# Hybrid decoder layer on one core: the last two pairs' expert rows summed on TensorE, the row planes loaded ahead of the last pair

## Chip, cores and metric

One core of a Trainium2 chip runs the whole layer in one launch. The metric is the device time of one execution in microseconds, as the median of several runs; less is better.

## What is computed

The layer takes x (512 tokens x 1024), mixes it by dilated attention and a spatial gating unit, projects and normalises it (LN1), and then runs a mixture of 32 experts of which each token uses two. The part around the change is the last line of the loop body:

```python
moe = hierarchical_moe(h, w_group, b_group, w_expert, b_expert, w_gate_up, w_down)
h = layer_norm(DEEPNORM_ALPHA * h + moe, ln2_g, ln2_b)
...
act = jax.nn.silu(a) * b * gate[:, g, :, None]
y = y + jnp.einsum('tef,efd->td', act, w_down[g])
```

So every token's output is LN2 of its own h plus the rows of its two experts, each weighted by its gate.

## The kernel before

Everything is float32. Experts are taken two at a time: 16 **pairs** (p = 0 to 15, `LAST` = 15), each with up to 64 tokens per expert, so that a pair fills 128 partitions. The tokens are four **tiles** of 128 (`NT`), and x, already normalised by LN1 and centred, stays in `x_sb`.

For each pair the loop (L1160 to L1209) does this. Its tokens' rows are gathered from `h_dram` into SBUF (POOL's indirect DMA, `gather`). TensorE transposes them (`transposed`) and multiplies them by the gate and up weights (`gate_up`, L905). ScalarE and VectorE form the gated activation `sa` (`gated`); TensorE transposes it and ScalarE copies it to `aT` (`act_transposed`); TensorE multiplies it by the down weights (`down`, L1112). The result y (128 slots x 1024) is copied out of PSUM by ScalarE with its row sums, centred on VectorE (L1121), and scattered by POOL's indirect DMA (L1122) into `y_dram`, which holds two planes of 512 rows: each token's first and second expert.

The last pair is not scattered. Its rows go to their tokens by a product: `one_hot(p)` (L1073) builds on POOL a 0/1 matrix G with one column per token, and `fin_y` multiplies G by y on TensorE in float32r (one instruction a product in the trace, where float32 has two). To keep the digits, y is split into a high half (ScalarE's copy) and a low half (VectorE's difference, L1117), and both are multiplied.

The weights come as 96 transfers of 1 MB, six a pair (four of gate/up, two of down), on SyncE's queue in order, into a ring of 21 buffers (`home(c)`, `wfill`). A transfer waits for the release of its buffer, and each DMA on this queue also waits for the landing of the one eight before it. Late in the kernel, buffers that have no next weight are used for other things: for ln2's gain and bias (`ln2`), for the planes (`rb`), for G and the low half (`spare`), for the outputs (`o_sb`).

ln2's gain and bias are spread over the partitions by small products (L1206) with ScalarE copies (L1208) in pairs 13 and 14, ahead of `act_transposed`.

**The end** (from L1211): the two planes are loaded back, eight transfers of 512 KB (L1216), after pair 14's scatter has landed. For each tile i and column half n, PSUM bank `fin[i, n]` collects: x by a product with the identity (`fin_x`, float32, L1158), pair 15's rows (`fin_y`, L1238), and the planes' rows, added up on POOL (L1244) and brought in by another identity product (`fin_rows`, L1245). The rows' means come from small products of G with the row sums `rs` (L1274). Then LN2: ScalarE squares with an accumulator (L1252), VectorE scales twice (L1257, L1264), SyncE stores (L1265). The order on each engine in this part is the order in which the code is written. A branch behind it serves experts with more than 64 tokens.

## Time and profile before

| What | Value |
|---|---|
| median of 3 runs | 501.38 us (501.13 to 502.98) |
| the profiled execution's own time | 501.38 us |
| its span, first to last instruction | 499.70 us |
| mean granted TensorE clock | 0.981 of full speed |
| TensorE products busy | 468.3 us (94%) |
| VectorE / ScalarE / POOL busy | 231.0 / 162.4 / 129.2 us |
| DMA | 141.18 MB, mean 283 GB/s |

The span is what the engines' instructions cover; the time of an execution holds 1.68 us more. Busy shares are means over stages that differ. In the last 60 us, which the change touches, only the rows by stage, the chain of waits and the landings of DMAs tell what sets the end.

### The profile page before, as it was taken

The page shows a single profiled execution, that of the slowest core. Times are in us where ns is not written, and L with a number is a line of the kernel's source. Part 1 is how long each engine was busy: PE and PEld are TensorE (multiplying, and loading weights), DVE is VectorE, ACT ScalarE, POOL GpSimd, SP SyncE. Part 2 cuts the span into 40 slices and gives each one's busy share as a digit, 9 for nine tenths or more (in the row PEclk, how much of TensorE's full clock was granted, in tenths as well). Part 3 has the DMA queues.
Part 4 walks back from the last instruction along what each step waited for, and adds up shares of the span by engine and source line. Part 5 has one row for each costly group of instructions (what it writes and reads, how often), then busy time and mean ns, then how long its engine had stood idle before and what let it go on. Part 6 is the DMA issues. An engine that isn't in the chain of part 4 may idle for free.

```text
span 499.7 us, 6653 instructions
## 1 busy us (share of the span) xinstructions
PE 468.3 (94%) x2322; PEld 280.8 (56%) x2322; DVE 231.0 (46%) x598; ACT 162.4 (33%) x366; POOL 129.2 (26%) x196
## 2 busy tenths in 40 slices
PE   7999999999899999987999999999998898799994
PEld 5788887888767678867843333333333233243351
DVE  3586637723477638798452222222234331010146
ACT  4543536241478632322112222222221121032243
POOL 4024345000296910344111211111110110000380
PEclk9999999999999999998899999999999999898998
DMA  8844231750298549585589999999999999998464
GB/s 262 288 125 114 63 121 42 221 200 0 65 402 254 190 161 364 201 282 245 169 324 378 428 419 419 419 420 422 421 420 419 420 426 419 419 423 373 151 241 171
DMA packets 40805, 141.18 MB, mean 283 GB/s; under 512 B 10508, under 2 KB 14656, under 8 KB 28993
## 3 DMA queue, kind: packets, MB, share of 16 engines
q1 hardware_dynamic: 35808, 130.71, 68.3%
q0 software_dynamic: 4960, 10.01, 5.5%
q8 instruction: 20, 0.33, 0.3%
q14 instruction: 17, 0.13, 0.1%
HBM read 131.78 MB, written 16.25 MB: 296 GB/s over the span
## 4 chain that ended last, share of the span: by engine, by line
PE 65%; DMA 25%; DVE 6%; ACT 1%; SPq 1%; issue 1%; POOL 1%; ACTq 0%; DVEq 0%
DMA wc<-in_w_gate_up 14%; PE acc L905 13%; DMA wc<-in_w_down 9%; PE acc L320 7%; PE acc L321 7%; PE acc L322 7%; PE acc L1112 6%; PE acc L920 3%; DMA x_sb<-in_x 2%; PE tp L1082 2%; PE acc L605 2%; PE tp L620 2%; PE acc L580 1%; PE acc L582 1%; PE acc L581 1%; PE sc L414 1%
## 5 line engine op out<-in xcount | busy, mean ns | idle before, releaser
L905 PE MATMUL acc<-wc,xTm 128*64 128x512 f32 x464 | 120.6, 608 | 8.3 <-DMA wc<-in_w_gate_up 8.0
L905 PEld LDWEIGHTS acc<-wc,xTm 128*64 128x64 f32 x464 | 33.3, 138 | 72.2 <-issue 52.8
L320 PE MATMUL acc<-w_hi,xTh 128*128 128x512 f32 x160 | 65.1, 407 | 0.8 <-ACT vs_sb L375 0.7
L321 PE MATMUL acc<-w_lo,xTh 128*128 128x512 f32 x160 | 62.9, 393 | 0.4 <-DVE w_lo L312 0.4
L322 PE MATMUL acc<-w_hi,xTl 128*128 128x512 f32 x160 | 62.8, 392 | 0.0
L1112 PE MATMUL acc<-wc,aT 128*64 128x512 f32 x240 | 60.0, 610 | 2.9 <-ACT aT L1097 2.9
L1122 POOL DMA_INDIRECT y_dram<-y,to x15 | 15.8, 1053 | 140.4 <-DVE xTm L1083 74.2
L1120 DVE TENSOR_SCALAR rs<-rs 128x1 f32<-128x1 f32 x15 | 3.2, 214 | 91.9 <-ACT y L1114 91.9
L312 DVE TENSOR_TENSOR w_lo<-w_raw,w_hi 128x512 fp32r<-128x512 f32 x40 | 28.2, 706 | 34.5 <-ACT w_hi L311 34.3
L311 ACT ACTIVATE w_hi<-w_raw 128x512 fp32r<-128x512 f32 x40 | 25.3, 634 | 53.2 <-PE acc L322 47.8
L1112 PEld LDWEIGHTS acc<-wc,aT 128*64 128x64 f32 x240 | 18.6, 140 | 34.3 <-issue 30.3
L1114 ACT ACTIVATE y<-acc 128x512 f32<-128x512 f32 x30 | 17.9, 597 | 60.7 <-PE acc L1112 44.3
L422 POOL TENSOR_TENSOR P<-P,st 128x128 f32<-128x128 f32 (+3 forms) x32 | 23.2, 749 | 50.8 <-DVE st L421 49.3
L320 PEld LDWEIGHTS acc<-w_hi,xTh 128*128 128x128 f32 x160 | 30.2, 189 | 7.8 <-ACT vs_sb L375 1.1
L321 PEld LDWEIGHTS acc<-w_lo,xTh 128*128 128x128 f32 x160 | 30.2, 189 | 6.9 <-DVE w_lo L312 1.4
L1088 DVE SCALAR_TENSOR_TENSOR sa<-sa,tg,acc 128x256 f32<-128x256 f32 x16 | 7.7, 479 | 56.9 <-ACT sa L1087 53.0
L322 PEld LDWEIGHTS acc<-w_hi,xTl 128*128 128x128 f32 x160 | 30.0, 188 | 6.7 <-DVE xTl L163 0.3
L897 POOL DMA_INDIRECT xg<-h_dram,ti x15 | 15.8, 1053 | 56.2 <-DVE ti L894 19.5
L1087 ACT ACTIVATE sa<-acc 128x256 f32<-128x256 f32 x16 | 6.2, 385 | 69.1 <-PE acc L905 69.1
L1082 PEld LDWEIGHTS tp<-ident,xg 128*128 128x128 f32 x120 | 15.1, 194 | 18.7 <-issue 8.9
L873 DVE TENSOR_TENSOR sel<-iota_v,slotp 128x1024 bf16<-128x1024 f32 (+2 forms) x23 | 22.5, 990 | 0.1
L420 ACT ACTIVATE P<-P,st 128x128 f32<-128x128 f32 (+3 forms) x32 | 17.9, 563 | 8.3 <-DVE st L418 8.2
(334 smaller groups left out, 781.0 us busy)
## 6 DMA issues: line engine op xcount, KB each, us to landing
wc<-in_w_gate_up SPq DMA_DIRECT2D x62, 1024.0 KB, 19.2
wc<-in_w_down SPq DMA_DIRECT2D x30, 1024.0 KB, 20.8
w_raw<-in_w_in SPq DMA_DIRECT2D x18, 512.0 KB, 3.7
y_dram<-zeros SPq DMA_DIRECT2D x8, 512.0 KB, 8.0
wo_raw<-in_w_out SPq DMA_DIRECT2D x16, 256.0 KB, 3.5
wc<-y_dram SPq DMA_DIRECT2D x8, 512.0 KB, 9.3
x_sb<-in_x SPq DMA_DIRECT2D x8, 256.0 KB, 9.4
h_dram<-x_sb SPq DMA_DIRECT2D x4, 512.0 KB, 3.0
```

Of the source, the lines that this page charges most:

```text
L311: act.activation(wh, raw, AF.Copy)
L312: dve.tensor_tensor(wl, raw, wh.bitcast(F32), op=ALU.subtract)
L320: pe.matmul(acc[i], xh, wh, start=(k == 0), stop=False)
L321: pe.matmul(acc[i], xh, wl, start=False, stop=False)
L322: pe.matmul(acc[i], xl, wh, start=False, stop=(k == KD - 1))
L420: act.activation(P[:, 0:n], P[:, 0:n], AF.Exp, bias=st4[:, 0:1], scale=-1.0, accum_out=st4[:, 1:2])
L422: pool_e.tensor_tensor(P[:, 0:n], P[:, 0:n], bc(st4[:, 2:3], [128, n]), op=ALU.mult)
L873: dve.tensor_tensor(sels[p][:, 2 * a:2 * b], bc(iota_v.rearrange("p a b -> p (a b)")[:, None, :], [128, n, 128]), bc(slotp[:, p, a:b].rear ...
L905: pe.matmul(gp[zs], xT[k // 4][:, k % 4, zs], w[k % 4 // 2][:, k % 2 * 512:k % 2 * 512 + 512], start=(k == 0), stop=(k == KD - 1))
L1082: pe.transpose(out=tp[:, j], in_=xv[:, kk * 4 + j], identity=ident)
L1112: pe.matmul(dp[n][zs], aT[:, c, zs], w[c][:, ns], start=(c == 0), stop=(c == 1))
L1114: act.activation(y0[:, ns], dp[n], AF.Copy, accum_out=rs[:, n:n + 1])
```

## The change

A constant `SUMMED` = 14 names the pair before the last. Pair 14's y is no longer scattered. VectorE centres it into a high half and writes the low half beside it (both float32r), and it reaches its tokens by products with its own one-hot matrix, as pair 15's does. So `fin_y` gets a third argument, the pair, and G becomes `Gs`, built for both pairs behind pair 14's down product.

The planes now only hold pairs 0 to 13. Their loads stand behind pair 13's `down`, right behind the last weights on SyncE's queue, in other free buffers. POOL's sums of the two planes (`rows_add`) are made for all four tiles first. For tiles 0 and 1 VectorE adds the rows to x in `x_sb` (`rows_x`), ahead of `down(LAST)`, so that one product of x brings both in; tiles 2 and 3 keep `fin_rows`.

The ln2 spreads of pairs 13 and 14 stand half ahead of and half behind `act_transposed`. Of the products of x, tile 2's move from ahead of the last gate/up product to the two places around `act_transposed`; those of tiles 0 and 1 move from there behind the last down product; tile 3's stay with its tile.

```diff
@@ -30,6 +30,7 @@
 NPAIR = NE // 2
 
 LAST = NPAIR - 1
+SUMMED = LAST - 1
 
 ATONCE = 9
 FF = 256
@@ -879,7 +880,7 @@
 
     def pair_out(p, ip):
 
-        if p < LAST:
+        if p < SUMMED:
             tos[p] = keep_p.tile([128, 1], I32, name="to", bufs=6)
             dve.scalar_tensor_tensor(tos[p], ip[:, 6:7], float(1 << 20), tgs[p][:, 0:1], op0=ALU.add, op1=ALU.add)
 
@@ -1070,7 +1071,7 @@
     xTm = [wk.tile([128, 2, 4, 128], F32, name="xTm", bufs=2) for _ in range(2)]
 
     def one_hot(p):
-        G = spare[:, 0:S]
+        G = late[0][:, (p - SUMMED) * S:(p - SUMMED + 1) * S]
         for i in range(NT):
             pool_e.tensor_scalar(G[:, i * 128:i * 128 + 128], iota_t, 128.0 * i, tgs[p][:, 0:1], op0=ALU.add, op1=ALU.is_equal)
         return G
@@ -1100,8 +1101,9 @@
     def down(p, aT, dp=None):
 
         dp = dp or [ps_acc() for _ in range(2)]
-        y = [wk.tile([128, D], F32R, name="y", bufs=1)] + ([spare[:, D:2 * D]] if p == LAST else [])
-        y0 = y[0].bitcast(F32)
+        y0 = wk.tile([128, D], F32R, name="y", bufs=1)
+        y = [y0, late[0][:, D:2 * D]] if p == LAST else [y0]
+        yf = y0.bitcast(F32)
         rs = mo.tile([128, 4], F32, name="rs", bufs=2)
         for n in range(2):
             ns = slice(n * 512, n * 512 + 512)
@@ -1111,18 +1113,26 @@
                     w = wq[6 * p + 4 + z]
                     pe.matmul(dp[n][zs], aT[:, c, zs], w[c][:, ns], start=(c == 0), stop=(c == 1))
             if p < LAST:
-                act.activation(y0[:, ns], dp[n], AF.Copy, accum_out=rs[:, n:n + 1])
+                act.activation(yf[:, ns], dp[n], AF.Copy, accum_out=rs[:, n:n + 1])
             else:
-                act.activation(y[0][:, ns], dp[n], AF.Copy, accum_out=rs[:, 2 * n:2 * n + 1])
-                dve.scalar_tensor_tensor(y[1][:, ns], dp[n], 1.0, y0[:, ns], op0=ALU.mult, op1=ALU.subtract,
+                act.activation(y0[:, ns], dp[n], AF.Copy, accum_out=rs[:, 2 * n:2 * n + 1])
+                dve.scalar_tensor_tensor(y[1][:, ns], dp[n], 1.0, yf[:, ns], op0=ALU.mult, op1=ALU.subtract,
                                          accum_out=rs[:, 2 * n + 1:2 * n + 2])
         if p < LAST:
             dve.tensor_scalar(rs[:, 2:3], rs[:, 0:1], rs[:, 1:2], -1.0 / D, op0=ALU.add, op1=ALU.mult)
-            dve.tensor_scalar(y0, y0, rs[:, 2:3], None, op0=ALU.add)
+        if p == SUMMED:
+            t = home(6 * LAST - 7).bitcast(F32R)
+            y = [t[:, z * D:z * D + D] for z in range(2)]
+            dve.tensor_scalar(y[0], yf, rs[:, 2:3], None, op0=ALU.add)
+            dve.scalar_tensor_tensor(y[1], yf, rs[:, 2:3], y[0].bitcast(F32), op0=ALU.add, op1=ALU.subtract)
+        elif p < SUMMED:
+            dve.tensor_scalar(yf, yf, rs[:, 2:3], None, op0=ALU.add)
             pool_e.indirect_dma_start(out=y_dram[:, :], out_offset=bass.IndirectOffsetOnAxis(ap=tos[p][:, 0:1], axis=0),
-                                      in_=y0, in_offset=None, bounds_check=2 * S - 1, oob_is_err=False)
+                                      in_=yf, in_offset=None, bounds_check=2 * S - 1, oob_is_err=False)
         wfill(6 * p + 6 + NSLOT)
         return y, rs
+
+    late = []
 
     def combine(G, y, i, n):
         cb = ps_s()
@@ -1166,9 +1176,6 @@
         if p == LAST - 2:
             ln2 = home(6 * LAST - 14).rearrange("p (a d) -> p a d", a=2)
             ln2_g, ln2_b = ln2[:, 0], ln2[:, 1]
-        if p == LAST:
-            for n in range(2):
-                fin_x(2, n)
         for k in range(KD):
             gate_up(p, [xTm[p % 2][:, kk] for kk in range(2)], k, gp)
             if k == 0:
@@ -1197,52 +1204,60 @@
             for kk in range(2):
                 transposed(xgs[(p + 1) % 2], xTm[(p + 1) % 2], kk)
             fetch(p + 3)
+            def ln2_spread(j):
+                a = p - LAST + 2
+                b = ps_s()
+                for z in range(2):
+                    r = 4 * a + 2 * j + z
+                    pe.matmul(b[:, 256 * z:256 * z + 256], ident[0:8, r:r + 1].to_broadcast([8, 128]), zeros[0:8],
+                              start=True, stop=True)
+                act.copy(ln2[:, a, hs[j]], b)
             if p >= LAST - 2:
-                a = p - LAST + 2
-                for j in range(2):
-                    b = ps_s()
+                ln2_spread(0)
+            aT = act_transposed(sa)
+            if p >= LAST - 2:
+                ln2_spread(1)
+            yr = down(p, aT)
+            if p == SUMMED - 1:
+
+                wfill(6 * NPAIR)
+                rb = []
+                for i in range(NT):
+                    t = home(6 * LAST - (15, 13, 12, 11)[i])
+                    t = [t[:, z * D:z * D + D] for z in range(2)]
                     for z in range(2):
-                        r = 4 * a + 2 * j + z
-                        pe.matmul(b[:, 256 * z:256 * z + 256], ident[0:8, r:r + 1].to_broadcast([8, 128]), zeros[0:8],
-                                  start=True, stop=True)
-                    act.copy(ln2[:, a, hs[j]], b)
-            down(p, act_transposed(sa))
-
-    rb = []
-    for i in range(NT):
-        t = home(6 * LAST - 13 + i)
-        t = [t[:, z * D:z * D + D] for z in range(2)]
-        for z in range(2):
-            sp.dma_start(out=t[z], in_=y_v[:, i, z])
-        rb.append(t)
-    spare = home(6 * LAST - 5).bitcast(F32R)
-    G = one_hot(LAST)
+                        sp.dma_start(out=t[z], in_=y_v[:, i, z])
+                    rb.append(t)
+            if p == SUMMED:
+                ys = [yr[0]]
+                late.append(home(6 * LAST - 6).bitcast(F32R))
+                Gs = [one_hot(q) for q in (SUMMED, LAST)]
     dp = [ps_acc() for _ in range(2)]
-    fin_x(0, 0)
-    aT = act_transposed(sa)
-    fin_x(1, 0)
-    fin_x(0, 1)
-    fin_x(1, 1)
-
-
-    o2 = [home(6 * LAST - z).rearrange("p (a d) -> p a d", a=2) for z in (9, 7)]
+
+
+    o2 = [home(6 * LAST - z).rearrange("p (a d) -> p a d", a=2) for z in (10, 9)]
     o_sb = [o2[i // 2][:, i % 2] for i in range(NT)]
-    sq = home(6 * LAST - 6).rearrange("p (a d) -> p a d", a=4)
+    sq = home(6 * LAST - 5).rearrange("p (a d) -> p a d", a=4)
     eps2 = mo.tile([128, 1], F32, name="eps2")
     pool_e.memset(eps2, EPS / ALPHA ** 2)
-    act.preload_act_table(AF.Sqrt)
     nx = mo.tile([128, NT], F32, name="nx")
 
-    def fin_y(i, n):
+    def fin_y(i, n, q):
         for z in range(2):
-            pe.matmul(fin[i, n], G[:, i * 128:i * 128 + 128], y[z][:, hs[n]], start=False, stop=False)
-
-    def fin_rows(i):
-
+            pe.matmul(fin[i, n], Gs[q][:, i * 128:i * 128 + 128], ys[q][z][:, hs[n]], start=False,
+                      stop=(q == 1 and z == 1 and i < 2))
+
+    def rows_add(i):
         for n in range(2):
             r = rb[i][0][:, hs[n]]
             pool_e.tensor_tensor(r, r, rb[i][1][:, hs[n]], op=ALU.add)
-            pe.matmul(fin[i, n], ident, r, start=False, stop=True)
+
+    def rows_x(i):
+        dve.tensor_tensor(x_sb[:, i], x_sb[:, i], rb[i][0], op=ALU.add)
+
+    def fin_rows(i):
+        for n in range(2):
+            pe.matmul(fin[i, n], ident, rb[i][0][:, hs[n]], start=False, stop=True)
 
     def ln2_scale(i):
 
@@ -1264,23 +1279,37 @@
             dve.scalar_tensor_tensor(o, fin[i, n], t[:, 4:5], ln2_b[:, hs[n]], op0=ALU.mult, op1=ALU.add)
             sp.dma_start(out=out_d[:, i, hs[n]], in_=o)
 
+
+    for i in range(NT):
+        rows_add(i)
+    fin_x(2, 0)
+    aT = act_transposed(sa)
+    act.preload_act_table(AF.Sqrt)
+    fin_x(2, 1)
+    for i in range(2):
+        rows_x(i)
     y, rs = down(LAST, aT, dp)
-    for i in range(NT - 1):
-        fin_y(i, 0)
+    ys.append(y)
+    for n in range(2):
+        fin_x(0, n)
+        fin_y(0, n, 0)
+    fin_y(0, 0, 1)
 
     fin[NT - 1, 0] = ps_acc()
     mb = fin[NT - 1, 1] = ps_acc()
     for i in range(NT):
-        pe.matmul(mb[:, 4 * i:4 * i + 4], G[:, i * 128:i * 128 + 128].bitcast(F32), rs, start=True, stop=True)
+        pe.matmul(mb[:, 4 * i:4 * i + 4], Gs[1][:, i * 128:i * 128 + 128].bitcast(F32), rs, start=True, stop=True)
     dve.tensor_reduce(nx, mb[:, 0:4 * NT].rearrange("p (i a) -> p i a", a=4), axis=AX.X, op=ALU.add)
     dve.tensor_scalar(nx, nx, -1.0 / D, None, op0=ALU.mult)
-    for i in range(NT - 1):
-        fin_y(i, 1)
-        fin_rows(i)
-    for n in range(2):
-        fin_x(NT - 1, n)
-        fin_y(NT - 1, n)
-    fin_rows(NT - 1)
+    fin_y(0, 1, 1)
+    for i in range(1, NT):
+        for n in range(2):
+            if i != 2:
+                fin_x(i, n)
+            fin_y(i, n, 0)
+            fin_y(i, n, 1)
+        if i > 1:
+            fin_rows(i)
     for i in range(NT):
         ln2_scale(i)
         ln2_out(i)
...
```

**On TensorE, behind the last down product.** `acc`, `sc` and `tp` are PSUM banks (`fin[i, n]`), and behind the arrow stand the two operands. y is pair 15's high half, `wc20` holds G and the low half, `wc14` tile 0's rows. Before:

```order
L1112 MATMUL acc_3898<-wc11_3670,aT_3904 64x512
L1238 MATMUL acc_3899<-y_3919,wc20_3892 128x512
L1238 MATMUL acc_3899<-wc20_3892 128x512
L1238 MATMUL sc_3906<-y_3919,wc20_3892 128x512
L1238 MATMUL sc_3906<-wc20_3892 128x512
L1238 MATMUL tp_3857<-y_3919,wc20_3892 128x512
L1238 MATMUL tp_3857<-wc20_3892 128x512
L1274 MATMUL acc_3940<-rs_3920,wc20_3892 128x4 x4
L1238 MATMUL acc_3908<-y_3919,wc20_3892 128x512
L1238 MATMUL acc_3908<-wc20_3892 128x512
L1245 MATMUL acc_3899<-wc14_3880,ident_87 128x512
L1245 MATMUL acc_3908<-wc14_3880,ident_87 128x512
```

Now (`wc0` holds pair 14's two halves, `wc1` the two one-hot matrices and pair 15's low half):

```order
L1114 MATMUL acc_3895<-wc11_3668,aT_3915 64x512
L1168 MATMUL acc_3936<-x_sb_86,ident_87 128x512
L1247 MATMUL acc_3936<-wc0_3862,wc1_3865 128x512 x2
L1168 MATMUL acc_3940<-x_sb_86,ident_87 128x512
L1247 MATMUL acc_3940<-wc0_3862,wc1_3865 128x512 x2
L1247 MATMUL acc_3936<-y_3922,wc1_3865 128x512
L1247 MATMUL acc_3936<-wc1_3865 128x512
L1301 MATMUL acc_3947<-rs_3923,wc1_3865 128x4 x4
L1247 MATMUL acc_3940<-y_3922,wc1_3865 128x512
L1247 MATMUL acc_3940<-wc1_3865 128x512
L1168 MATMUL sc_3956<-x_sb_86,ident_87 128x512
L1247 MATMUL sc_3956<-wc0_3862,wc1_3865 128x512 x2
```

Tile 0 is started by its product of x and pair 14's rows, behind the last down product; the three tiles' products of pair 15 no longer come together ahead of the means.

**On VectorE, from pair 14's activation to the row means.** `sa` is the gated activation, `x_sb` x, `acc` the down product's two banks. Before:

```order
L1088 SCALAR_TENSOR_TENSOR sa_3809<-sa_3809,tg_3607,acc_3792 128x256
L1083 COPY xTm_2592<-tp_3812 128x512
L1120 TENSOR_SCALAR rs_3840<-rs_3840 128x1
L1121 TENSOR_SCALAR y_3839<-y_3839,rs_3840 128x1024
L1088 SCALAR_TENSOR_TENSOR sa_3877<-sa_3877,tg_3696,acc_3856 128x256
L1117 SCALAR_TENSOR_TENSOR wc20_3892,rs_3920<-acc_3897,y_3919 128x512
L1117 SCALAR_TENSOR_TENSOR wc20_3892,rs_3920<-acc_3898,y_3919 128x512
L1275 TENSOR_REDUCE nx_3918<-acc_3940 128x4
```

Now:

```order
L1089 SCALAR_TENSOR_TENSOR sa_3819<-sa_3819,tg_3607,acc_3802 128x256
L1084 COPY xTm_2592<-tp_3822 128x512
L1122 TENSOR_SCALAR rs_3850<-rs_3850 128x1
L1126 TENSOR_SCALAR wc0_3862<-y_3849,rs_3850 128x1024
L1127 SCALAR_TENSOR_TENSOR wc0_3862<-y_3849,rs_3850,wc0_3862 128x1024
L1089 SCALAR_TENSOR_TENSOR sa_3891<-sa_3891,tg_3694,acc_3874 128x256
L1256 TENSOR_TENSOR x_sb_86<-x_sb_86,wc12_3790 128x1024
L1256 TENSOR_TENSOR x_sb_86<-x_sb_86,wc14_3793 128x1024
L1119 SCALAR_TENSOR_TENSOR wc1_3865,rs_3923<-acc_3894,y_3922 128x512
L1119 SCALAR_TENSOR_TENSOR wc1_3865,rs_3923<-acc_3895,y_3922 128x512
L1302 TENSOR_REDUCE nx_3901<-acc_3947 128x4
```

Pair 14's centring (L1126) is followed by its low half (L1127), and two additions of rows to x (L1256) stand between pair 15's activation and its low half.

## Rows read from the trace of the kernel before

**Rows 1.** Busy time by stage over the last 60 us: start:end, length, then each engine's busy us.

```profile
450.00:460.00 10.00, 9.21 (x40) 4.20 (x38) 1.08 (x2) 2.52 (x5) 0.00 (x0) 0.86 0.93 390
...
475.00:482.00 7.00, 7.00 (x34) 3.67 (x34) 1.94 (x6) 1.38 (x4) 5.63 (x5) 1.00 1.00 396
```

**Rows 2.** The chain of work that ended last: start us, us, engine, tile, line, instructions.

```profile
453.71 1.93 PE sc L1206 x8
...
455.67 0.59 ACT wc L1208
...
456.86 5.35 PE acc L1112 x16
462.21 1.91 PE tp L1158 x4
...
475.23 3.58 PE acc L1112 x16
...
481.96 1.72 PE acc L1245 x4
483.67 0.47 PE sc L1238 x2
...
490.67 0.87 PE acc L1245 x2
```

**Rows 3.** DMA issues on SyncE in order of time, the last cut to one issue.

```profile
446.14 2.82 SPq L534 DMA_DIRECT2D wc<-in_w_down  x2
470.16 4.53 SPq L1216 DMA_DIRECT2D wc<-y_dram  x8
...
473.76 0.92 SPq L1216 DMA_DIRECT2D wc<-y_dram  x1
```

**Rows 4.** DMA issues: KB each, us from issue to landing; last one the last plane's.

```profile
wc<-in_w_down SPq DMA_DIRECT2D x1, 1024.0 KB, 21.0
y_dram<-y,to POOLq DMA_INDIRECT x1, 8.4
...
wc19g<-in_w_down SPq DMA_DIRECT2D x2, 512.0 KB, 21.6
...
wc<-y_dram SPq DMA_DIRECT2D x1, 512.0 KB, 10.0
```

**Rows 5.** Stage table again, 468 to 470; the last two columns are DMA share and GB/s.

```profile
468.00:470.00 2.00, 2.00 (x12) 0.69 (x10) 0.00 (x0) 0.00 (x0) 0.64 (x2) 1.00 0.05 20
```

**Rows 6.** POOL's instructions in order of time, 448 to 478.

```profile
448.30 0.97 POOL L1122 DMA_INDIRECT y_dram<-y,to  x1 [19.85 <-DVE y L1121]
...
465.75 2.85 POOL L1075 TENSOR_SCALAR wc<-iota_t,tg 128x128 fp32r<-128x128 f32 x4
...
475.38 2.49 POOL L1244 TENSOR_TENSOR wc<-wc 128x512 f32<-128x512 f32 x2 [6.75 <-DMA wc<-y_dram]
```

**Rows 7.** VectorE: one group over the whole span (mean ns), then instructions near 480.

```profile
L873 DVE TENSOR_TENSOR sel<-iota_v,slotp 128x1024 bf16<-128x1024 f32 x13 | 15.8, 1219 | 0.0
...
471.61 0.48 DVE L1088 SCALAR_TENSOR_TENSOR sa<-sa,tg,acc 128x256 f32<-128x256 f32 x1 [7.63 <-ACT sa L1087]
...
479.58 0.69 DVE L1117 SCALAR_TENSOR_TENSOR wc<-acc,y 128x512 fp32r<-128x512 f32 x1 [0.97 <-ACT y L1116]
480.20 0.08 DVE L1117 DVE_READ_ACCUMULATOR wc<-acc,y 128x1 f32 x1
```

**Rows 8.** VectorE, then POOL, in order of time near 211 us (routing).

```profile
210.84 1.26 DVE L916 TENSOR_TENSOR S<-sel 128x128 f32<-128x128 bf16 x1
...
210.66 1.29 POOL L737 TENSOR_TENSOR x_sb<-x_sb,ln_g 128x512 f32<-128x512 f32 x1 [5.94 <-ACT x_sb L734]
212.03 1.55 POOL L738 TENSOR_TENSOR x_sb<-x_sb,ln_b 128x512 f32<-128x512 f32 x1
```

**Rows 9.** Stage table around pair 14's down product; the granted clock stands third from the end.

```profile
453.80:457.20 3.40, 2.60 (x12) 1.75 (x14) 0.37 (x1) 2.08 (x4) 0.00 (x0) 1.00 0.94 392
457.20:460.70 3.50, 3.50 (x10) 0.96 (x8) 0.00 (x0) 0.38 (x1) 0.00 (x0) 0.51 0.80 330
```

More of the change, by code (lines that the diff above doesn't have):

```diff
@@ L1296, in layer @@
             for n in range(2):
-                combine(G, y, i, n)
-            dve.tensor_tensor(x_sb[:, i], x_sb[:, i], rb[i][0], op=ALU.add)
+                for q in range(2):
+                    combine(Gs[q], ys[q], i, n)
+            if i > 1:
+                rows_x(i)
         with tc.For_i(0, NE, 1) as e:
```

## The prediction, made before the change was run

> **What bounds the kernel now.** I read three things: the stage table, the chain of work that ended last, and the DMA landings. The profiled execution is itself the median run: 501.38 us (runs 501.13 to 502.98), a span of 499.70 us plus 1.68 us around it. Every shift of the last output that I work out below is added to 501.38.
>
> The stage table of the last 60 us shows TensorE busy for 9.21 of 10 us from 450 and for all 7.00 us from 475 [rows 1]. The chain agrees: over these 60 us it is a row of TensorE pieces with waits of a microsecond at most, so TensorE's own work sets the end. The reader should see four stations: pair 14's down product at 456.86, the last gate/up product behind two products of x (462.21 + 1.91 = 464.1), the last down product at 475.23 (done 478.81), and the last half of tile 3's rows at 490.67, done 491.54 [rows 2]. From there to the end (one ScalarE square, two VectorE steps, the output's transfer) nothing is edited.
>
> What this chain doesn't show is how late DMA data lands, because TensorE arrives later still. SyncE issues pair 15's last weight at 446.14 + 2.82 - 0.33 = 448.63 [rows 3]. It lands 21.0 us later, at **469.64** [rows 4], against a use from 475.23. In the last 2 us before 470 DMA is busy by a share of 0.05, which is one of 16 engines [rows 5]. So one DMA engine lags behind the rest by microseconds. A transfer is only complete when that engine has done its part.
>
> **The change part by part.** *Spreads.* Pairs 13 and 14 each split the ln2 products around the transposes of the activation. For pair 14 the stretch from 453.71 to 456.86 (3.15 us) holds two halves of 0.97, transposes of 0.45 and a ScalarE wait [rows 2]. Now the second half follows ScalarE's copy of the first: 0.97 + 0.59 + 0.97 and an estimated 0.16 of latencies = 2.69, so 0.46 gained. Pair 13's is the same edit in a place where TensorE waited less; between 0 and 0.46 I take 0.2. Together 0.66.
>
> *Products of x.* Tile 2's two leave the place ahead of the last gate/up product: 1.91. Of the four behind it, two remain, so 2 x 0.86 = 1.72 goes (0.86 is half of the 1.72 of two such products at 481.96 [rows 2]). The last down product thus ends 0.66 + 1.91 + 1.72 = 4.29 earlier, at 474.5. Pair 15's weights allow it: gate/up would start at 461.5 and need its second half's weights at about 465.0 (its last one landed near 464.6, two issues of 2.49 us ahead of the last), and the down product would start at 470.9, 1.3 us behind 469.64.
>
> *Behind the down product.* Four products of x come in (+3.44) and the four row products of tiles 0 and 1 leave (-3.44). Pair 14's rows add 16 products at 0.235 (a pair takes 0.47 [rows 2]): +3.76. With nothing late, the last piece would end 4.29 - 3.76 = 0.5 us earlier than 491.54. That is all the TensorE work can give.
>
> *Removed elsewhere.* Pair 14's scatter leaves POOL and its queue, and with it the wait that held the planes' loads to 470.16 [rows 3]. Its y is split on VectorE instead (two passes of 1024 columns, at most 2 x 0.69 each [rows 7]), ahead of 471.61, where VectorE had idled for 7.63 us [rows 7]; uncovered it would cost up to 2.8. POOL makes eight one-hot tiles where four took 2.85 [rows 6], from about 453, done by 459, ahead of any plane.
>
> *The planes.* The eight 512 KB loads are now issued from when pair 13's scatter has landed (448.30 + 8.4 = 456.7 [rows 4]), behind the last weights on the same queue. Does that bring them in by 470? A 512 KB weight half issued into the full queue took 21.6 us, as long as a whole 1024 KB one [rows 4]: a transfer waits for what lies ahead of it. On the lagging engine that is the last weight, until 469.64. From there a plane takes between 1.25 us (the last two 1024 KB weights were issued 2.49 apart, at the pace of landings [rows 3]) and 1.70 (all eight planes from the first issue at 470.16 to 473.76 + 10.0 = 483.76 [rows 3, 4]). I take 1.4, as the last six planes came between 475.38 and 483.76 [rows 4, 6]. Tile 0's two planes land at 472.4, tile 1's at 475.2, tile 2's at 478.0. Before, tile 0's were in by 475.38 and nothing waited for them on TensorE.
>
> *The new wait.* VectorE must add tile 0's and tile 1's rows to x, and both additions stand in its queue **ahead** of the low half of pair 15's y, for which the row means and every product of that low half wait. Each needs POOL's sum first: 2.49 a tile [rows 6]. An addition of 128x1024 with two inputs is taken at 1.22 [rows 7], bounded by 2 x 0.69. Without contention: 475.2 + 2.5 + 1.2 = 478.9, then the two low halves 1.4 and 0.05 of latency: 480.4. Before, they were done at 480.28 [rows 7].
>
> *POOL against VectorE.* A VectorE addition that started 0.18 us after a POOL one took 1.26 us for 128 columns and ended 0.15 us after POOL's did; the next POOL one then ran 1.55 instead of 1.29 [rows 8]. So two-input work on the two engines excludes each other here. Tile 0's addition (474.9 to 476.1) then holds up POOL's sum of tile 1, which ends at 478.7. Tile 2's planes are there by then, and if POOL's next piece gets in first, tile 1's addition runs from 479.95 to 481.15 and the low halves end at 482.6. The first hold-up I count in full, the second by half: 482.0. The Trainium skill (Advanced Engine Details and Errata, VectorE Performance Modes) names only VectorE's two-port modes as blocking GpSimd and lists no such mode for an addition of two tensors. By it the low halves would end at 480.4; the row speaks against it, so it is a rival.
>
> *The end.* Before, the low halves' end at 480.28 was followed by the last piece of TensorE at 491.54. Between them lay the means, tile 0's last product, and 9.58 us from 481.96 [rows 2]. Now the stretch from tile 0's last product holds tile 1 (3.60), tile 2 (3.60) and tile 3 up to its first half of rows (1.72 + 1.88 + 0.87 = 4.47): 11.67, which is 2.09 more, as tile 1's and 3's x products and pair 14's rows come behind the wait. The sum is (482.0 - 480.28) + 2.09 = **+3.8 us: 505.2 us**. Bounds: 1.25 a plane without contention gives 479.8 and +1.6; contention in full gives 482.6 and +4.4.
>
> *The clock.* Pair 14's down product took 5.35 where the last took 3.58 [rows 2]; its granted clock was 0.51 (the lower level, 1.2 GHz) after 3.4 us of transposes and spreads with 0.80 of idling [rows 9]. TensorE would now idle about 1.6 us at 474.5 and over 2 us at 479, so a fall is likely. It costs 0 if it lies in the waits, up to 5.35 - 3.58 = 1.77 behind them. I take 0, since the first wait comes nearly 10 us ahead of the dense part, and keep 1.7 for the range: 503.0 to 507.5 for this case. The fall at 457 may vanish, but TensorE would only wait longer for the same planes.
>
> **The rivals.** *Planes in time (not slower).* If the planes don't queue behind the lagging engine, they take about 9 to 10 us from their issue as before, so tile 1's pair is in by 470, POOL's sums by 473, and VectorE's additions lie ahead of pair 15's y. Then TensorE's work decides: 501.38 - 0.5 = **500.9**. For it: nearly all DMA engines are free before 470 [rows 5]. Against: the 21.6 us of the half transfer. It decides if tile 1's planes land before about 471. *The same with the clock kept*: if the low stretch at 457 goes too, the last weights at 469.64 set the down product, which ends at 473.3: 1.2 less, **499.7**. *Late planes without contention*: 480.4, so +2.2, **503.6** (+1.6 to +3.4 by the two paces). *The change doesn't do what it says*: the loads could be held back by SyncE itself, as each waits for the landing of the transfer eight before it; then the last goes out only at 469.7. That serves tile 3, whose rows are needed after 488: no cost.
>
> **How the numbers follow.** Late planes with contention 0.62, late planes without 0.13, planes in time 0.20, the same with the clock kept 0.05. About 0.5% (2.5 us) is what a measurement of this kernel can tell from no change: slower means above 503.89, faster below 498.87. The first case is above with 0.57 of its 0.62, the second with 0.04; planes in time are inside with 0.16 and faster with 0.04, by a clock that stays up elsewhere; the last 0.03 and 0.02. Sums: slower 0.61, same 0.33 (0.05 + 0.09 + 0.16 + 0.03), faster 0.06. The range runs from 500.4, which takes in most of planes in time, to 507.2, near the end of the likeliest case; some 0.17 lies outside.
>
> **What would show it.** Right: the planes' landing behind 470 although issued at 457; VectorE idle from about 473 until a POOL sum; its two additions ending near 476 and 480 to 481; TensorE idle twice between 474.5 and 482; its last piece at about 495. Wrong: tile 1's planes in by 471 and TensorE without a gap behind the down product; or the two additions next to POOL sums at 1.2 us each. The whole forecast falls if a plane can overtake a weight on the lagging engine, or if that engine is on time in the new run.

## The result and the profile after

The changed kernel takes **505.26 us** (median of 8 runs, 503.80 to 506.91) against 501.57 us for the kernel before, measured with it (8 runs): a ratio of **1.0061, 95% interval 1.0037 to 1.0086**. It is slower, by about what was forecast. The profiled execution took 504.57 us, of which 502.9 are the span; that is 3.2 us over the 501.38 and 499.70 of before.

The page of the changed kernel, busy time by engine (us, share of the span, instructions):

```profile
span 502.9 us, 6669 instructions
PE 469.1 (93%) x2330; PEld 283.1 (56%) x2330; DVE 235.8 (47%) x600; ACT 162.0 (32%) x366; POOL 132.6 (26%) x199
```

TensorE is busy for only 0.8 us more than before; the span grew by four times that. The time was lost in waiting or at a lower clock, and the stage table says where. Busy time in the stage from 475, same columns as [rows 1]:

```profile
475.00:482.00 7.00, 5.14 (x14) 3.00 (x14) 5.21 (x6) 0.06 (x1) 7.00 (x5) 0.76 0.06 22
```

In the stage from 475, where TensorE was busy for all 7.00 us before, it is busy for 5.14, at a mean granted clock of 0.76. DMA is busy by a share of only 0.06, about one of 16 engines, with the last planes; POOL is busy throughout. The chain of work that ended last (start us, us, engine, tile, line, instructions) starts in DMA and passes over VectorE:

```profile
459.40 14.85 DMA wc<-y_dram
...
474.42 2.31 DVE x_sb L1256
...
476.86 1.52 PE acc L1168 x2
...
481.87 0.79 PE acc L1301 x8
482.65 0.57 PE acc L1247 x2
...
493.90 0.87 PE acc L1260 x2
```

The last half of tile 3's rows ends at 493.90 + 0.87 = 494.77, where [rows 2] has 490.67 + 0.87 = 491.54: 3.23 later. Everything behind it is as before.

Now the links one by one. DMA issues on SyncE (start us, us, queue, line; the last is the eighth plane alone), then what its queue waited for (us in total, times, longest):

```profile
445.88 2.82 SPq L535 DMA_DIRECT2D wc<-in_w_down  x2
456.09 13.49 SPq L1229 DMA_DIRECT2D wc<-y_dram  x8
...
469.27 0.32 SPq L1229 DMA_DIRECT2D wc<-y_dram  x1
```

```profile
SPq L1229 <- DMA wc<-in_w_gate_up: 6.2, 3, 2.1
SPq L1229 <- DMA wc<-in_w_down: 4.2, 2, 2.1
```

The planes are issued from 456.09, but each issue from the fourth on waits for an earlier transfer to land; the eighth for the last weight. So the last weight landed just ahead of 469.27. The eighth took 10.0 us from issue to landing (the last one before took 10.0 too [rows 4]), so it was in at 479.3. The planes ahead of it took longer: tile 1's second, issued at 459.40, took the 14.85 us of the chain above and was in at 474.25. POOL and VectorE (start us, us, engine, line, operation, in brackets the idle time before it and what ended it):

```profile
471.90 11.85 POOL L1253 TENSOR_TENSOR wc<-wc 128x512 f32<-128x512 f32 x8 [17.27 <-DMA wc<-y_dram]
```

```profile
474.42 2.30 DVE L1256 TENSOR_TENSOR x_sb<-x_sb,wc 128x1024 f32<-128x1024 f32 x1 [5.10 <-POOL wc L1253]
477.87 2.28 DVE L1256 TENSOR_TENSOR x_sb<-x_sb,wc 128x1024 f32<-128x1024 f32 x1 [1.16 <-POOL wc L1253]
480.07 0.68 DVE L1119 SCALAR_TENSOR_TENSOR wc<-acc,y 128x512 fp32r<-128x512 f32 x1
...
480.68 0.68 DVE L1119 SCALAR_TENSOR_TENSOR wc<-acc,y 128x512 fp32r<-128x512 f32 x1
481.29 0.08 DVE L1119 DVE_READ_ACCUMULATOR wc<-acc,y 128x1 f32 x1
```

POOL had waited 17 us for tile 0's planes. Each VectorE addition took 2.3 us beside POOL's sums. And TensorE (same columns), with a table of stretches below it:

```profile
470.67 3.65 PE L1114 MATMUL acc<-wc,aT 128*64 128x512 f32 x16
476.86 1.52 PE L1168 MATMUL acc<-x_sb,ident 128*128 128x512 f32 x2 [2.54 <-DVE x_sb L1256]
...
479.04 1.91 PE L1168 MATMUL acc<-x_sb,ident 128*128 128x512 f32 x2
...
481.71 0.95 PE L1301 MATMUL acc<-rs,wc 128*128 128x4 f32 x8
...
483.06 1.02 PE L1168 MATMUL sc<-x_sb,ident 128*128 128x512 f32 x2
```

```profile
475.00:478.00 3.00, 1.14 (x3) 0.59 (x3) 1.84 (x2) 0.06 (x1) 3.00 (x3) 0.90 0.11 42
478.00:481.00 3.00, 3.00 (x6) 1.55 (x5) 3.00 (x4) 0.00 (x0) 3.00 (x2) 0.53 0.03 10
```

The last down product ends at 474.3, 4.5 us earlier than the 478.81 of before. TensorE then stands still for 2.54 us until VectorE has added tile 0's rows, and runs tile 0's products at a granted clock of 0.53 (the lower level, 1.2 GHz): two products of x take 1.91 where 1.02 is the rule further on. From 476.86 to the start of tile 1 at 483.06 lie 6.20 us. From the end of the down product to the last piece lie 494.77 - 474.32 = 20.45 us, where the kernel before had 491.54 - 478.81 = 12.73. The difference, 7.72, is made up of pair 14's rows (16 products at 0.235, 3.76), the wait (2.54) and the slow clock (6.20 where 4.57 is the time at the full clock, as runs below show: 1.63), 7.93 in all, less 0.20 by which the row means took less (0.79, before 0.99). What was gained ahead of the down product is gone, and 3.2 us with it.

### The profile page after: what moved, and what is told of

The parts are those of the page before. It is cut to its first block, busy times and chain, and to the rows that moved or that the text cites. A ratio compares the mean times of both kernels' runs of the same rounds, so it can differ in the third digit from the quotient of the medians.

```text
span 502.9 us, 6669 instructions
## 1 busy us (share of the span) xinstructions
PE 469.1 (93%) x2330; PEld 283.1 (56%) x2330; DVE 235.8 (47%) x600; ACT 162.0 (32%) x366; POOL 132.6 (26%) x199
## 4 chain that ended last, share of the span: by engine, by line
PE 50%; DMA 39%; DVE 6%; SPq 1%; ACT 1%; issue 1%; POOL 1%; DVEq 0%; ACTq 0%; POOLq 0%
DMA wc<-in_w_gate_up 21%; DMA wc<-in_w_down 12%; PE acc L321 7%; PE acc L322 7%; PE acc L323 7%; PE acc L906 5%; PE acc L921 3%; DMA wc<-y_dram 3%; DMA x_sb<-in_x 2%; PE acc L606 2%; PE tp L621 2%; PE acc L581 1%; PE acc L1114 1%; PE acc L583 1%; PE acc L582 1%; PE acc L1168 1%
```

## The experiments

Twelve kernels were run in four groups; each is compared with the kernel before on its own chip (median 501.45, 501.64, 501.61 and 501.86). **Theory:** late planes, two engines that exclude each other, a wait, and the price of the wait. **Rivals:** TensorE's own new products cost the time; the planes could be made early; one of the two additions alone is to blame.

One measure needs a word. The time at which SyncE issues the last two weights differs by almost 4 us between executions (446.14 before, 445.88 in the changed kernel, 445.10 and 449.03 in two below). Where planes set the end, all that follows shifts with it, so for such kernels I also give the **tail**: the end of TensorE's last piece minus that issue. It is 494.77 - 445.88 = 48.89 in the changed kernel.

### The changed kernel again

> The changed kernel once more, beside the three that follow. Expected: about 3.7 us above the kernel before (505.3 against 501.6), with VectorE's two additions at about 2.3 us each, pair 15's low halves ending near 481.4 and TensorE's last half of tile 3's rows near 494.8.

Measured: 506.31 us (6 runs), ratio 1.0110 (1.0076 to 1.0145). VectorE's additions took 2.27 and 2.28, and the tail is 48.85. The traced shape repeats; the two medians of this kernel differ by 1.05 us. In one thing the trace differs: pair 14's down product ran at the full clock here (3.65 us instead of 5.35), and nothing was gained by it, since TensorE then waited 2.92 us for tile 0's rows instead of 2.54.

### No planes at all

```diff
-                        sp.dma_start(out=t[z], in_=y_v[:, i, z])
+                        pool_e.memset(t[z], 0.0)
```

> The planes' eight loads are replaced by POOL memsets in the same place, so the rows of pairs 0 to 13 are left out of the output; every sum and product on them stays. Late-planes theory: TensorE goes on behind the down product without a wait (two additions done long before), low halves end near 476.3, tile 3's last half near 490.8, time about 4 us below the changed kernel: 501.2 (500.5 to 502). Rival, the 16 added products and the products of x moved behind the down product are the price: within 1 us of 505.3. Rival, the lower clock behind the down product: in between, if the clock falls there without a wait as well.

Measured: 507.77 us (6 runs), 1.0148 (1.0108 to 1.0188): a miss, by a new wait. With nothing to wait for, POOL ran its sums early, from 460.28, just when VectorE had to centre pair 14's y (VectorE's and POOL's rows):

```profile
462.47 8.21 DVE L1126 TENSOR_SCALAR wc<-y,rs 128x1024 fp32r<-128x1024 f32 x1
```

```profile
460.28 9.84 POOL L1253 TENSOR_TENSOR wc<-wc 128x512 f32<-128x512 f32 x8
```

A pass of 0.76 us took 8.21, until 0.6 us after the end of POOL's sums (470.12), and pair 15's activation stood behind it. So this kernel says nothing of the planes yet.

### No planes, and POOL's sums held back

```diff
-                        sp.dma_start(out=t[z], in_=y_v[:, i, z])
+                        pool_e.memset(t[z], 0.0)
...
+    held = mo.tile([128, 1], F32, name="held")
+    pool_e.tensor_copy(held, ys[0][1][:, D - 1:D].bitcast(F32))
     for i in range(NT):
         rows_add(i)
```

> no_planes again without its side effect (POOL's sums, free of the loads, had run at 460 to 470 and held up VectorE's centring of pair 14's y by 8 us): POOL's sums now wait for the low half of pair 14's y. The rows of pairs 0 to 13 are again left out of the output. Late-planes theory: sums from about 465, both additions done by 474, no wait of TensorE behind the down product, no fall of the clock there, low halves at about 476.3, tile 3's last half near 490.7; time 0.5 us below the kernel before: 501.0 (500.3 to 501.8). Rival, the added and moved products of TensorE are the price: above 504.5.

Measured: 501.26 us (12 runs), 0.9995 (0.9970 to 1.0019). All of TensorE's new products are still there, and nothing is lost: tile 0's first product follows the last down product (done 477.25) without idle time.

```profile
477.18 1.12 PE L1168 MATMUL acc<-x_sb,ident 128*128 128x512 f32 x2
```

The 16 products of pair 14's rows are not the price; that rival falls. The additions, again beside POOL and slow (472.17 to 475.99 for both), are done before the down product ends.

### All rows by products

```diff
-                      stop=(q == 1 and z == 1 and i < 2))
+                      stop=False)
...
-    for i in range(2):
-        rows_x(i)
...
     fin_y(0, 1, 1)
+    fin_rows(0)
...
-        if i > 1:
-            fin_rows(i)
+        fin_rows(i)
```

> VectorE's two additions are taken out and tiles 0 and 1 get their row products on TensorE back, so TensorE has four more products of 0.86 (3.44 us). Late-planes theory: no wait, so tile 3's last half comes at 490.8 + 3.4 = 494.2, time about 0.5 us below the changed kernel (504.7), in spite of 3.4 us more work. Rival, TensorE's work is the price: 505.3 + 3.4 = 508.7.

Measured: 505.34 us (12 runs), 1.0057 (1.0036 to 1.0077). TensorE does 3.44 us more here than in the changed kernel, waits nowhere behind the down product (472.46 to 476.1, tile 0 from 476.05), and the time is the same. What VectorE's additions save on TensorE, the way to them costs again.

### Planes ahead of the last two weights

```diff
-        for src in srcs[len(wq):n]:
+        for src in srcs[len(wq):min(n, limit[0])]:
...
+    limit = [6 * NPAIR - 2]
...
-                wfill(6 * NPAIR)
                 rb = []
                 for i in range(NT):
+                    if i == 2:
+                        limit[0] = 6 * NPAIR
+                        wfill(6 * NPAIR)
```

> The planes of tiles 0 and 1 are put ahead of pair 15's two down weights on SyncE's queue, nothing else. Theory, a transfer waits on the lagging DMA engine for all that was issued ahead of it: tile 0's sum on POOL starts about 5 us earlier (near 467 instead of 471.9), the two down weights land about 5 us later (472 and 474.5), so the last down product can only start near 474.5 instead of 470.7, and the time stays within 1.5 us of the changed kernel (505). Rival, the planes are late by themselves (slow reads of the row buffer, or SyncE's waits): tile 0's sum still starts near 472 and the down product near 471.

Measured: 507.45 us (4 runs), 1.0112 (1.0074 to 1.0151), about 1 us above the band that was expected. The order on SyncE's queue, then TensorE and VectorE:

```profile
455.87 1.75 SPq L1232 DMA_DIRECT2D wc<-y_dram  x4
458.06 2.81 SPq L535 DMA_DIRECT2D wc<-in_w_down  x2
463.05 5.24 SPq L1232 DMA_DIRECT2D wc<-y_dram  x4
```

```profile
473.11 1.04 PE L1115 MATMUL acc<-wc,aT 128*64 128x512 f32 x2 [1.54 <-DMA wc<-in_w_down]
475.46 3.65 PE L1115 MATMUL acc<-wc,aT 128*64 128x512 f32 x14 [1.30 <-DMA wc<-in_w_down]
```

```profile
470.66 2.33 DVE L1259 TENSOR_TENSOR x_sb<-x_sb,wc 128x1024 f32<-128x1024 f32 x1 [0.51 <-POOL wc L1256]
474.15 1.22 DVE L1259 TENSOR_TENSOR x_sb<-x_sb,wc 128x1024 f32<-128x1024 f32 x1 [1.16 <-POOL wc L1256]
```

Four planes pushed ahead of two weights bring POOL's first sum from 471.90 to 468.12, and now the weights are late: the down product waits 1.54 and 1.30 us for them. What is late is thus settled by place in the queue. The first addition ran beside POOL's sums (468.12 to 474.12) and took 2.33; the second ran beside an idle POOL, 1.22.

### VectorE adds both planes itself

```diff
-    for i in range(NT):
+    for i in range(2, NT):
         rows_add(i)
...
         rows_x(i)
+        dve.tensor_tensor(x_sb[:, i], x_sb[:, i], rb[i][1], op=ALU.add)
```

> VectorE adds both planes of tiles 0 and 1 to x itself (two additions a tile), and POOL sums only tiles 2 and 3. Contention theory: the four additions take 1.1 to 1.2 us each instead of 2.3, tile 0's x is ready at 474.3 instead of 476.7, TensorE hardly waits and its clock stays up, low halves end at 478.3 instead of 481.4, tile 3's last half near 491.5; time about 3.2 us below the changed kernel (502.3). Rival, the planes' lateness alone counts and contention costs nothing: the additions take 1.2 with and without POOL, and the time stays within 1 us of the changed kernel.

Measured: 500.78 us (12 runs), 0.9977 (0.9957 to 0.9997), better than expected. VectorE, of its four additions the first and the last, and TensorE:

```profile
471.90 1.22 DVE L1256 TENSOR_TENSOR x_sb<-x_sb,wc 128x1024 f32<-128x1024 f32 x1 [1.22 <-DMA wc<-y_dram]
...
475.73 1.23 DVE L1291 TENSOR_TENSOR x_sb<-x_sb,wc 128x1024 f32<-128x1024 f32 x1
```

```profile
472.04 3.65 PE L1114 MATMUL acc<-wc,aT 128*64 128x512 f32 x16
475.62 1.12 PE L1168 MATMUL acc<-x_sb,ident 128*128 128x512 f32 x2
...
480.19 1.02 PE L1168 MATMUL sc<-x_sb,ident 128*128 128x512 f32 x2
```

The planes come as late as ever, but POOL is silent, so an addition takes 1.22, and it needs one plane, not two and a sum. TensorE has no wait and keeps its clock (1.00 from 475 to 481): tile 0 takes 480.19 - 475.62 = 4.57 us instead of 6.20. POOL's sum between the planes and VectorE was the costly link. How much of the gain is the sum itself (2.5 us a tile) and how much the hold-up beside it (1.1 us an addition) this run doesn't separate.

### The second addition behind the low halves

```diff
-    for i in range(2):
-        rows_x(i)
+    rows_x(0)
     y, rs = down(LAST, aT, dp)
+    rows_x(1)
```

> One line moves: tile 1's addition stands behind the low halves of pair 15's y on VectorE instead of ahead. Late-planes theory: the low halves no longer wait for tile 1's addition and end at 476.7 + 1.4 = 478.1 instead of 481.4; tile 1's product of x waits at most 0.4 us; time about 2.9 us below the changed kernel (502.4). If the contention alone were the price and the place in the queue free: no difference. If TensorE's work is the price: no difference.

Measured: 505.45 us (10 runs), 1.0073 (1.0042 to 1.0105): a miss. The low halves were done before the second addition, as intended, and nothing came of it; the tail is 497.87 - 449.03 = 48.84. Tile 0's products again went at the lower clock, 6.17 us from 479.99 to 486.16:

```profile
479.99 1.10 PE L1168 MATMUL acc<-x_sb,ident 128*128 128x512 f32 x2 [2.94 <-DVE x_sb L1256]
...
486.16 1.02 PE L1168 MATMUL sc<-x_sb,ident 128*128 128x512 f32 x2
```

### The same, with TensorE kept busy

```diff
     rows_x(1)
+    fin[0, 0] = ps_acc()
+    for _ in range(3):
+        pe.matmul(fin[0, 0], ident, x_sb[:, 3, hs[0]], start=True, stop=True)
```

> low_half_first with three products of x (0.86 us each) into tile 0's bank, overwritten by its first real one, behind the down product while TensorE waits. Clock theory: low_half_first gained little because the products of tile 0 ran at half the clock after the wait (6.3 us from tile 0's first product to its last instead of 4.7); with the wait filled the clock stays at its upper level and these take 4.7, so the time is about 1.7 us below low_half_first and 2 to 3 us below the changed kernel: 503.3. Rival, the clock falls whatever TensorE did just before: no gain, or 0.3 lost where the fill outlasts the wait.

Measured: 504.65 us (9 runs), 1.0071 (1.0046 to 1.0096). In the trace the clock stays at 1.00 from 478 to 481, tile 0 takes 4.57 us (478.91 to 483.48), and the tail is 495.18 - 448.05 = 47.13: 1.7 less than without the filling, as expected. TensorE behind the filling:

```profile
478.91 1.12 PE L1168 MATMUL acc<-x_sb,ident 128*128 128x512 f32 x2
...
483.48 1.02 PE L1168 MATMUL sc<-x_sb,ident 128*128 128x512 f32 x2
```

The forecast of the time, 503.3, missed. The median is only 0.8 lower than without the filling, and its ratio is the same within the interval (1.0071, 1.0073): the gain is seen in one trace and not in the times.

### TensorE kept busy, and nothing else

```diff
     y, rs = down(LAST, aT, dp)
+    fin[0, 0] = ps_acc()
+    for _ in range(3):
+        pe.matmul(fin[0, 0], ident, x_sb[:, 3, hs[0]], start=True, stop=True)
```

> The changed kernel with only the filling: three overwritten products of x (six instructions, 2.84 us) behind the last down product, so that TensorE does not stand still while it waits for tile 0's addition; the second addition stays ahead of the low halves. Theory of two chains of about equal length: in the changed kernel TensorE's slow products of tile 0 (6.20 us from 476.86 to 483.06, where 4.57 is their time at the full clock) and VectorE's low halves (done 481.37, 0.34 ahead of the means at 481.71) ended together. Then filling alone leaves the low halves in the way: the granted clock is 1.00 behind the wait, tile 0's first products are done over 1 us earlier, and TensorE then waits about 1 us for the low halves; the last piece of TensorE ends 48.3 to 48.6 us after the issue of the last two weights (changed kernel 48.85 to 48.89), about 505 us in time. Rival, the clock alone set the end and the low halves were never near it: no wait ahead of the means, the last piece 47.1 to 47.5 us after that issue, about 503.7 us.

Measured: 505.81 us (12 runs), 1.0074 (1.0055 to 1.0093), tail 48.71, 0.1 above the first theory's and 1.2 above the rival's. TensorE, then the chain that ended last:

```profile
477.16 1.13 PE L1168 MATMUL acc<-x_sb,ident 128*128 128x512 f32 x2
...
481.21 0.51 PE L1247 MATMUL acc<-wc 128*128 128x512 f32 x1 [0.91 <-DVE wc L1119]
```

```profile
477.17 1.07 POOL wc L1253
...
478.27 0.06 DVE x_sb L1256
478.33 2.14 issue
480.47 1.31 DVE wc L1119 x4
...
481.82 1.05 PE acc L1304 x8
```

With the clock at 1.00 TensorE comes to the low halves sooner and waits 0.91 us for them: the second addition now binds, and the chain is the one of the prediction. So there are **two chains of about equal length** behind the late planes: TensorE's slow products of tile 0, and the second addition with the low halves. Taking away one alone changes next to nothing (tails 48.84 and 48.71 against 48.89); taking away both gives 1.7 us. This rests on one trace of each kernel (two of the changed one, whose tails agree within 0.04); the ratios of the three, 1.0073, 1.0074 and 1.0071, don't tell them apart.

### The split spreads alone, in the kernel before

```diff
...
             if p >= LAST - 2:
...
+                ln2_spread(0)
+            aT = act_transposed(sa)
+            if p >= LAST - 2:
+                ln2_spread(1)
+            down(p, aT)
-            down(p, act_transposed(sa))
```

> The kernel before with the ln2 spreads alone split around the activation's transposes. By the sum: 0.66 us of TensorE gained in pairs 13 and 14, 500.8. Rival, a place that waits for weights or a fall of the clock takes it back: 501.4, no difference.

Measured: 501.60 us (12 runs), 1.0006 (0.9986 to 1.0026). No gain can be measured in the time. In the trace pair 14's stretch from the first spread to the down product takes 458.67 - 455.81 = 2.86 us, where the kernel before has 456.86 - 453.64 = 3.22: 0.36 of the 0.46 that the prediction put on it.

### Rows of tiles 2 and 3 on VectorE instead of 0 and 1

```diff
-    fin_x(2, 0)
+    fin_x(0, 0)
     aT = act_transposed(sa)
...
-    for i in range(2):
-        rows_x(i)
...
     fin_y(0, 1, 1)
+    fin_rows(0)
+    rows_x(2)
...
+        if i == 1:
+            ln2_scale(0)
+            ln2_out(0)
+            rows_x(3)
```

> The changed kernel with the additions on VectorE for the tiles that come last: tiles 2 and 3 get their rows added to x behind the row means and behind tile 0's LN2, tiles 0 and 1 keep row products behind their tile's other products. The work of TensorE is that of the changed kernel. Theory: nothing that TensorE waits for depends on a plane before 479, so its work alone decides, 0.5 us below the kernel before: 501.0. Rival, the additions now hold up VectorE's LN2 and come back at the end: 502.5 or more.

Measured: 500.85 us (12 runs), 0.9990 (0.9968 to 1.0011). POOL's sums start as late as ever (471.92), but TensorE goes from the down product (470.30) to tile 0 (473.88) without a wait, since the first thing it needs of the planes comes at 476.94:

```profile
473.88 1.19 PE L1247 MATMUL acc<-wc,wc 128*128 128x512 f32 x4
...
476.94 1.88 PE L1260 MATMUL acc<-wc,ident 128*128 128x512 f32 x4
```

The tile that takes an addition decides, not the addition. Here VectorE's first addition also got in 0.33 us ahead of POOL's next sum, and the turn is the other way round: the addition takes 1.23, and POOL's two pieces 3.27 instead of 2.5:

```profile
479.41 1.23 DVE L1256 TENSOR_TENSOR x_sb<-x_sb,wc 128x1024 f32<-128x1024 f32 x1 [2.47 <-POOL wc L1253]
```

```profile
479.74 3.27 POOL L1253 TENSOR_TENSOR wc<-wc 128x512 f32<-128x512 f32 x2 [0.36 <-issue]
```

### Three tiles' rows on VectorE, plane by plane

On top of the kernel in which VectorE adds both planes itself, tile 3's planes are loaded ahead of tile 2's and also added by VectorE, one behind the low halves, one behind the row means; POOL sums only tile 2, held back until then.

```diff
-                for i in range(NT):
+                for i in (0, 1, 3, 2):
...
     ys.append(y)
+    plane_x(3, 0)
...
     fin_y(0, 1, 1)
+    plane_x(3, 1)
+    held = mo.tile([128, 1], F32, name="held")
+    pool_e.tensor_copy(held, x_sb[:, 3, D - 1:D])
+    rows_add(2)
...
-        if i > 1:
+        if i == 2:
             fin_rows(i)
```

> vector_sums carried on: tile 3's planes are loaded ahead of tile 2's and added to x by VectorE as well (the first behind the low halves, the second behind the row means), so tile 3 has no row products; POOL sums tile 2 alone, held until VectorE's last addition. Theory: TensorE loses 1.72 us of products at the very end, VectorE takes 1.2 to 2.4 more where it idled between 478 and 482; time 1.5 us below vector_sums: 499.4. Rival, VectorE becomes the bound of the last stage (its LN2 work of about 3 us a tile starts later): 500.8 or more, no gain over vector_sums.

Measured: **499.33 us** (12 runs), 0.9964 (0.9938 to 0.9990). It beats both kernels. That it beats the kernel with both planes on VectorE for two tiles only is not shown: the intervals of the two ratios (0.9964 and 0.9977) overlap. All six additions take 1.22 to 1.23, and tile 3 ends with its last product of y at 488.65, in the traced execution, the fastest of the twelve:

```profile
487.71 0.94 PE acc L1248 x4
```

## Why the prediction was right, step by step

**Late planes: right, a little too late.** The last weight was put at 469.64 and landed just ahead of 469.27; the eight planes were in 479.3 - 469.3 = 10.0 us later, 1.25 each, where 1.4 was taken. That is the lower of the two bounds. Tile 0's planes were in at 471.9 (forecast 472.4), tile 1's at 474.25 (475.2). That they queue behind the weights is shown by the kernel with four planes ahead of them, where the weights became late.

**The last down product** was to end at 474.5 and ended at 474.3. The cut ahead of it, 4.29 in the forecast, measures 4.5, with what two executions differ by anyway; the 0.66 of the spreads can't be told from nothing in the time of a run of their own, though the trace of that run has 0.36 of pair 14's 0.46.

**POOL against VectorE: right in kind, half of it too small.** The step "the first hold-up I count in full, the second by half" was too small in its second part, and it left one hold-up out. The forecast let tile 0's addition start ahead of POOL's next piece, take 1.2 us (474.9 to 476.1) and hold up POOL; in fact both additions took 2.3 us, 1.1 over their 1.22. POOL's next pieces start at once (474.37 and 477.80), 0.05 and 0.07 us ahead of VectorE, which starts only on the signal that the sum is ready; so in this kernel the addition comes second both times. For the same reason TensorE's first wait, forecast at about 1.6 us, was 2.54. The Trainium skill (SBUF — State Buffer, Who interferes with whom) says that a VectorE instruction with two SBUF inputs contends with a GpSimd instruction that reads SBUF; the 2.30 beside POOL and the 1.22 without it agree. The rival of late planes without contention is excluded by the same rows.

**The low halves** were to end at 482.0 and ended at 481.37: faster planes and the fuller hold-up nearly cancel, which is luck. With the measured end the sum reads (481.37 - 480.28) + 2.09 = +3.18, against +3.23 in the trace.

**The clock: the step that failed.** I took 0 for it, because "the first wait comes nearly 10 us ahead of the dense part". It cost 6.20 - 4.57 = 1.6 us, and it lay not in a wait but on tile 0's products. The sum did not suffer, because this loss ran beside the second addition and the low halves and was as long as they; that the two are equally long is luck. So the chain on which the forecast rested is not the one that ended last: the low halves were done at 481.37, 0.3 us ahead of the means that need them (481.71). TensorE's second idle time, forecast at over 2 us near 479, did not come; its slow products filled it. The run with TensorE kept busy shows that chain binding by itself; the run with the low halves first shows the other.

**The chances.** *Planes in time* had 0.20 at 500.9: its time was right (501.26 with no planes to wait for), its condition was not. *The same with the clock kept* is answered by the second run of the changed kernel: the low stretch at 457 was gone, and TensorE only waited longer for the same planes, as the prediction said. *Late planes without contention* is out by the rows above. *Loads held back by SyncE* came true, the eighth until 469.27, and cost nothing, as said: it is tile 3's.

**What stays open.** That it is one DMA engine that lags is read from the shares alone (0.05 [rows 5], and 0.03 from 478 to 481 in the changed kernel); why it lags no run here shows. That the filled kernel's median gained 0.8 where its trace gained 1.7, and its ratio nothing, is not settled either.

## What to carry to other kernels

Take a transfer's arrival from what lies ahead of it in its queue, not from its issue: loads issued 14 us earlier came only 3.5 us earlier (tile 0's planes 471.9, before 475.38). Work that depends on late data belongs to the tile that is used last, and two-input additions on VectorE go badly beside POOL's; give one of the two engines the whole sum. Before you credit a wait with the loss, look for a second chain of the same length: here, in one trace of each kernel, each of two hid what the other cost, and only removing both showed it.

## What the runs showed of the hardware

A one-input pass of VectorE over 128x1024 float32 (0.76 us alone) took 8.21 us beside POOL's sums that followed one another without a gap, held for some six pieces of 1.26; the two-input additions were held for one piece only, 1.1 us, and where the addition started first, POOL's piece was held instead (3.27 us for two pieces instead of 2.5). TensorE's clock fell to the lower level behind a single wait of 2.54 us and cost 1.6 us; with 2.84 us of overwritten products in the wait it stayed at 1.00. And in the traces of the kernel before and the changed one alike pair 14's down product ran slowly (5.35 us), while in the second trace of the changed kernel it took 3.65 us at a clock of 1.00: that fall does not come in every execution.
